# Attention stage of a two-layer backbone: one order for all units, the filler cut around the first transpositions

## The chip, the core and the metric
The kernel runs on one core of a Trainium2 chip. The metric is the device time of one execution, in microseconds (us); the time of a kernel is the median of several runs. Five engines work side by side, each through its own list of instructions: TensorE (PE, matrix products and transpositions), VectorE (DVE), ScalarE (ACT), GpSimd (POOL), and SyncE (SP), which here issues the DMAs. Results of TensorE go into PSUM, eight banks of 128 x 512 float32; everything else works from SBUF.

## The reference
Two layers over 1024 latent and 256 context tokens of width 1024: the first mixes tokens by differential attention, the second by a state-space scan; a squared-ReLU MLP follows each. The change lies in the attention:

```python
q_l = apply_rope(heads_qk(q_l), cos, sin) * scale       # 8 heads, two components of 64
k_all = jnp.concatenate([k_c, k_l], axis=1)             # 256 context + 1024 latent keys
def attend(q, k, v):
    s = jnp.einsum('bqhcd,bkhcd->bhcqk', q, k).astype(jnp.float32)
    p = jax.nn.softmax(s, axis=-1)
    w = p[:, :, 0] - lam * p[:, :, 1]                    # two softmaxes, one subtracted
    o = jnp.einsum('bhqk,bkhe->bqhe', w.astype(v.dtype), v)
    return rmsnorm(o, subln_g) * (1.0 - lambda_init)
y_lat = jnp.einsum('bte,ed->btd', o_l, w_o)
```
Context queries read the 256 context keys alone. All is float32.

## The kernel before
Products that need float32 accuracy are made of three (`mm3`, lines 132 to 134): both operands are held as a coarse part and a remainder, and three of the four cross products are summed in PSUM. `split` (lines 137, 138) makes the two parts: ScalarE copies the coarse one, VectorE or GpSimd subtracts it.

`phase_b` runs the attention in 72 units, nine for each head (the profile shows it from 224.1 to 858.5 us), and then five rounds without a unit of its own (n = 72 to 76). Unit 0 holds the 256 context queries against 256 keys, units 1 to 8 hold 128 latent queries each against 1280 keys. Each unit has these steps:

- `scores`: 8 or 12 products into banks 0 to 4 (lines 575, 581).
- `maxima` on VectorE (590, 594): reads the banks, writes the raw weights to SBUF with their extremes.
- `exps` on ScalarE (601, 604): two exponentials, one for each of the two softmaxes, with their sums.
- `combine` on VectorE (612, 613, 615): the weighted difference. L615 takes two operands from SBUF.

The weights have to stand the other way round for the product with the values. So TensorE transposes the weights of the unit before, in three parts (`w_part`, 622 and 627): four blocks into bank 5 (part 0), two into the second half of bank 6 (part 1), four into bank 7 where the unit has no group of filler, else into bank 5 again (part 2). Unit 0 of a head transposes unit 8 of the head before. The weights of a unit 0 have one part, of four blocks. `w_evac` empties a part into the coarse and remainder halves of `wT`: part 0 directly, by ScalarE (635) and VectorE (636); parts 1 and 2 by a copy on ScalarE (640) into one of three raw buffers and two steps of GpSimd (641 coarse, 642 remainder).

TensorE's work beside that, called filler, is of two kinds. `values` multiplies two finished units with the values: 30 products of 256 columns into the first half of bank 6, in units 1, 4, 6 and 8 (6 of them in unit 2 for the context queries); `pair_out` copies the sum out (725) and `pair_sums` adds its squares (732). And units 0, 1, 2, 3, 5 and 7 (table `AHEAD`) carry a projection group of the next head's queries or keys, 24 products into bank 7, of 512 columns, in units 1 and 3 of 256. The group is emptied at the unit's end: 256 columns by 523 and 524, 512 columns by 528 and 529, and then, one step at a time at the places of `next_post`, four DMAs and the sine (534, GpSimd), the sum (537, VectorE), the split and store (137, 138). Head 7 has no next head; it carries groups of the output product, 18 products of 512 columns, from n = 65 on.

PE, DVE, ACT and POOL run in written order (`manual_schedule`); the DMAs on SyncE are placed by the scheduler. The written order of a unit is: scores, maxima, all of `values`, then the three parts, each followed by its emptying, by one exponential (parts 0 and 1), by the combination (part 1), and by a slice of the group (`FILLS`, or products 0-2, 3-5, 6-7; `FILL_FIRST` puts unit 5's first slice ahead of part 0). In units with 30 products of values (`late`), all emptyings stand behind both exponentials and the combination. In the other units part 0 is emptied ahead of the first exponential, and part 1's copy stands ahead of the second.

Among the other work in the same lists: `norm_pair` (765 and a split, 137) of a finished head in units 7 to 2, `norm7` (801, 803) in the last head.

Of the kernel before, what the change touches and what calls it, by code (L numbers as in the profile page):

```python
# [70 lines left out]
class Prog:  # L71
# [575 lines left out]


    AHEAD = {0: (1, 0), 1: (1, 2), 2: (1, 1), 3: (0, 2), 5: (0, 0), 7: (0, 1)}
    FILLS = {1: (0, 0, 4, 8), 3: (0, 4, 8, 8)}  # L650
    FILL_FIRST = (5,)

    def b_start(self):

# [25 lines left out]
    def phase_b(self):  # L680
# [11 lines left out]
        pb = self.bank(6)  # L692
# [21 lines left out]
        def values(h, pair):  # L714
            V = loaded[h, "v"]
            last = 2 if pair == 0 else 10
            for kt in range(last):
                self.mm3(pb[:, 0:256], V[0][:, kt], V[1][:, kt], self.wT[0][:, kt], self.wT[1][:, kt],
                         kt == 0, kt == last - 1)

        hst = self.fv(7, 3, 8, 10)

# [33 lines left out]
        def norm_load(h, pair):  # L756
            i = nbuf.next()
            nloaded.append(i)
            self.dma(nbufs[i][0], self.od[h, :, 256 * pair : 256 * pair + 256])
            self.dma(nbufs[i][1], self.rsd[h, 2 * pair : 2 * pair + 2].rearrange("a b -> (a b)").partition_broadcast(128))  # L760

        def norm_pair(h, pair):
            i = nloaded.pop(0)
            (nob, nrb), (nhi, nlo) = nbufs[i], nsplit[i]
            nc.vector.scalar_tensor_tensor(nob, nob, self.sg, nrb, ALU.mult, ALU.mult)
            self.split(nhi, nlo, nob, nc.gpsimd)
            for j, t in enumerate((nhi, nlo)):
                self.dma(self.on[h, j, :, 256 * pair : 256 * pair + 256], t.bitcast(F32))
# [91 lines left out]
        prev, todo, sums, post, tail, run7 = None, [], [], [], [], []  # L860
# [4 lines left out]
        def next_post():  # L865
            f = post.pop(0) if post else None
            if f:
                f()

        ready = []  # L870

        def evac():
            while ready:
                self.w_evac(*ready.pop(0))

        with self.manual():
            for n in range(72 + 5):
                h, u = units[n] if n < 72 else (8, 9)
                front = n < 72
                groups = []  # L880
                pv = todo.pop(0)[1:] if todo and todo[0][0] == n else None
                late = pv and pv[1]
                parts = 3 if prev and prev[1] else 1 if prev else 0
                if front and n - 6 >= 9 and (n - 6) % 9 < 5 and (n - 6) // 9 < 7:
                    norm_load((n - 6) // 9 - 1, (n - 6) % 9)
                if h == 7 and u > 5:
                    load6(u)
                if front:
                    K = loaded[h, 'k', 0], loaded[h, 'k', 1]
                    pair = (u + 1) // 2  # L890
                    Q = loaded[h, pair]
                    s0 = hst[:, 0, h]
                    p, sn, sm = (p0.next(), p1), self.stat.next(), self.stat.next()
                    if u == 5 and h < 7:
                        load_v(h + 1)
                        load_k(h + 1, 0)
                        load_k(h + 1, 1)
                    if u % 2 == 0 and u < 8 and (h, pair + 1) not in loaded:
                        load_q(h, pair + 1)
                    if h < 7:  # L900
                        groups = [self.proj_group(h + 1, *a, wts[a[0]]) for a in (self.AHEAD[u],)] if u in self.AHEAD else []
                    self.scores(u, Q, K)
                    if u == 7 and h < 7:
                        load_q(h + 1, 0)
                    if u == 8 and h < 7:
                        load_q(h + 1, 1)
                    self.maxima(u, p, sm)
                if front:
                    if h < 7:
                        if u == 0:  # L910
                            qsplit = self.proj_weights(h + 1, 0)
                        if u == 5 and h < 6:
                            ksplit = self.proj_weights(h + 2, 1)
                if 65 <= n < 75:
                    groups = [wo_group(wo_order[n - 65])]
                fills = [[], [], []]
                if h >= 7 and groups:
                    fills = [groups[0][0][i : i + 2] for i in (0, 2, 4)]
                elif groups:
                    a = self.FILLS.get(u, (0, 3, 6, 8))  # L920
                    fills = [groups[0][0][a[i] : a[i + 1]] for i in range(3)]
                if pv:
                    values(*pv)
                if u in self.FILL_FIRST and front and h < 7:
                    for f in fills[0]:
                        f()
                    fills[0] = []
                for part in range(3):
                    if part < parts:
                        tb = pb[:, 256:512] if part == 1 else self.bank(7 if part == 2 and not groups else 5)  # L930
                        t = self.w_part(prev[1], prev[2], part, tb)
                        ready.append((*t, part == 0))
                    if not late or part == 2:
                        evac()
                    if part == 1:
                        next_post()
                    if front and part < 2:
                        self.exps(u, part, p, sm, s0, sn)
                    if front and part == 1:
                        if n - 7 >= 9 and (n - 7) % 9 < 5 and (n - 7) // 9 < 7:  # L940
                            norm_pair((n - 7) // 9 - 1, (n - 7) % 9)
                        self.combine(u, p, s0, sn)
                    if late and part == 1:
                        evac()
                    if part == 0:
                        todo7, run7 = run7, []
                        for f in todo7:
                            f.pop(0)()
                            if f:
                                run7.append(f)  # L950
                    if part == (2 if n < 73 else 0):
                        while sums and sums[0][0] <= n:
                            sums.pop(0)[1]()
                    for f in fills[part]:
                        f()
                if front and u == 0:
                    next_post()
                if pv:
                    pair_out(*pv)
                    sums.append((n + 1, lambda a=pv: pair_sums(*a)))  # L960
                    if pv[0] == 7:
                        tail.append((n + 1, pv[1]))
                next_post()
                if groups:
                    rest = groups[0][1]
                    rest[0]()
                    post += rest[1:]
                if h < 7 and u in (0, 2):
                    wts[0] = qsplit(u // 2)
                if h < 6 and u in (6, 7):  # L970
                    wk = ksplit(u - 6)
                if u == 8 and h < 6:
                    wts[1] = wk
                if front and u % 2 == 0:
                    todo.append((n + 2, h, pair))
                prev = (h, u, p[0]) if front else None
                if 0 < h < 8:
                    if u == 3:
                        newton = norm_calc(h - 1)
                    elif u == 4:  # L980
                        newton()
                    elif u == 5:
                        norm_rows(h - 1)
                if n == 72:
                    self.raw = Ring([self.wv(8, 1024), self.wv(12, 1024)])
                    self.wo_raws = [self.wo_load(3, 0), self.wo_load(0, 1)]
                if n == 60:
                    wload6(0)
                if n == 62:
                    wload6(1)  # L990
                    wload6(2)
                    wsplit6(0)
                if h == 7:
                    beside7(u)
                    if u > 5:
                        norm6(u)
                if tail and tail[0][0] == n:
                    run7.append(list(norm7(tail.pop(0)[1])))
# [1586 lines left out]
```

## Time and profile before

| | us |
|---|---|
| median of 3 runs | 2853.43 (2853.11 to 2854.3) |
| the profiled execution | 2849.43 |
| its span | 2847.7 |
| attention stage in it (224.1 to 858.5) | 634.4 |
| TensorE busy in that stage | 603.7 |
| VectorE, ScalarE, GpSimd busy in that stage | 509.8, 370.8, 411.7 |
| TensorE waiting for L636 in that stage | 23.9 in 16 waits |

The profile shows one execution. A row of a timeline has the start in us, the busy time, the engine, the line of the code, the operation, output and inputs with their shapes, how many equal instructions it joins, and, in brackets, the idle time of the engine ahead of it with the instruction that ended it. A row of stretches has the stretch, its length, and the busy time of PE, weight loading, DVE, ACT and POOL, then the granted clock of TensorE as a share of full speed, the share of DMA and GB/s. A row of waits has who waited for whom, the total, how often, and the longest. Matmuls of TensorE overlap: the distance between two starts, not the busy time of one, is what each adds. In the rows, F holds the weights and raw copies, R the queries, keys, values and `wT`, H and W projection weights and inputs, PS is PSUM.

### The profile page before, as it was taken

To read this page: it belongs to the slowest core of one execution; us is meant where nothing else is said; L and a number is where in the kernel's file an instruction comes from. 1 tells how busy PE (TensorE), PEld (TensorE's weight loads), DVE (VectorE), ACT (ScalarE), POOL (GpSimd) and SP (SyncE) were. 2 spreads that over 40 slices of the span, in tenths; PEclk is the share of its full clock that TensorE was granted. 3 is DMA by queue.
4 is the path that set the end of the run, shared out by engine and by line. 5 is a ranking of instruction groups with operands and counts; after the bars stand their busy time and mean duration, and the time that the engine had idled before them with its cause. 6 is when DMAs were issued, how large, how long until landed. Compare 5 with 4: busy or idle time off the path is not lost. (4 is left out here: it accounts for less than half of the span.)

```text
span 2847.7 us, 43378 instructions
## 1 busy us (share of the span) xinstructions
PE 2723.8 (96%) x15229; PEld 2284.8 (80%) x15229; DVE 2017.4 (71%) x2984; ACT 1368.4 (48%) x2583; POOL 1031.7 (36%) x901
## 2 busy tenths in 40 slices
PE   6999999999999999999999999889999999999999
PEld 4688888888877887778877878788887778878887
DVE  6366788888873676667698878799543697768466
ACT  3425555555653753333444445487344633344443
POOL 3314666666663600000030013588121143335414
PEclk9999999999999999999999999899999999999999
DMA  9956556555835359886799877579742244476544
GB/s 271 322 176 199 147 164 177 173 172 163 259 100 177 133 182 315 292 303 221 246 318 303 275 240 259 169 228 309 233 155 97 69 162 158 155 247 226 167 132 142
DMA packets 414823, 586.30 MB, mean 206 GB/s; under 512 B 41870, under 2 KB 260236, under 8 KB 411404
## 3 DMA queue, kind: packets, MB, share of 16 engines
q1 hardware_dynamic: 414604, 583.52, 63.8%
q8 instruction: 120, 1.97, 0.3%
q14 instruction: 99, 0.81, 0.1%
HBM read 396.38 MB, written 182.82 MB: 203 GB/s over the span
## 5 line engine op out<-in xcount | busy, mean ns | idle before, releaser
L132 PE MATMUL PS<-H 128*128 128x512 f32 x1072 | 420.9, 394 | 3.2 <-ACT H L137 1.9
L134 PE MATMUL PS<-H 128*128 128x512 f32 x1072 | 418.1, 391 | 2.0 <-DVE H L2260 1.3
L133 PE MATMUL PS<-H 128*128 128x512 f32 x1072 | 418.4, 390 | 0.0
L132 PE MATMUL PS<-H,R 128*128 128x512 f32 (+1 forms) x828 | 308.7, 375 | 4.4 <-ACT R L137 1.2
L133 PE MATMUL PS<-H,R 128*128 128x512 f32 (+1 forms) x828 | 299.0, 361 | 0.2 <-POOL H L138 0.2
L134 PE MATMUL PS<-H,R 128*128 128x512 f32 (+1 forms) x828 | 298.1, 361 | 0.0
L132 PEld LDWEIGHTS PS<-H 128*128 128x128 f32 x1072 | 201.6, 188 | 51.4 <-issue 6.2
L134 PEld LDWEIGHTS PS<-H 128*128 128x128 f32 x1072 | 201.6, 188 | 44.9 <-DVE H L2260 1.7
L133 PEld LDWEIGHTS PS<-H 128*128 128x128 f32 x1072 | 201.5, 188 | 40.5
L604 ACT ACTIVATE F<-F,stat 128x1280 f32<-128x1280 f32 x128 | 174.3, 1362 | 100.5 <-DVE F L594 100.3
L137 ACT ACTIVATE H<-U 128x640 fp32r<-128x640 f32 x216 | 131.9, 674 | 175.1 <-PE PS L133 145.6
L132 PE MATMUL PS<-R,H 128*128 128x512 f32 x520 | 208.4, 402 | 3.3 <-ACT H L137 3.3
L137 ACT ACTIVATE R<-W 128x512 fp32r<-128x512 f32 (+1 forms) x184 | 128.6, 707 | 168.8 <-PE PS L133 98.1
L134 PE MATMUL PS<-R,H 128*128 128x512 f32 x520 | 206.1, 398 | 1.8 <-DVE H L138 1.8
L133 PE MATMUL PS<-R,H 128*128 128x512 f32 x520 | 205.2, 395 | 0.0
L138 DVE TENSOR_TENSOR H<-U,H 128x640 fp32r<-128x640 f32 x216 | 165.4, 799 | 52.5 <-ACT H L137 51.3
L138 DVE TENSOR_TENSOR H<-W,H 128x512 fp32r<-128x512 f32 (+1 forms) x137 | 124.4, 918 | 102.0 <-ACT H L137 101.5
L594 DVE TENSOR_SCALAR_CACHE_REDUCE F<-PS 128x1280 f32<-128x1280 f32 x128 | 185.2, 1483 | 8.0 <-PE PS L581 7.7
L137 ACT ACTIVATE H<-W 128x512 fp32r<-128x512 f32 (+2 forms) x158 | 95.5, 613 | 189.0 <-PE PS L133 116.2
L132 PEld LDWEIGHTS PS<-H,R 128*128 128x128 f32 x828 | 157.7, 191 | 31.9 <-issue 4.1
L134 PEld LDWEIGHTS PS<-H,R 128*128 128x128 f32 x828 | 157.3, 190 | 25.6 <-issue 0.8
L641 POOL TENSOR_SCALAR R<-F 128x256 fp32r<-128x256 f32 (+1 forms) x128 | 126.2, 986 | 136.9 <-ACT F L640 123.1
(530 smaller groups left out, 6845.7 us busy)
## 6 DMA issues: line engine op xcount, KB each, us to landing
W<-in_mlp_w SPq DMA_DIRECT2D x176, 256.0 KB, 3.1
U<-Aa SPq DMA_DIRECT2D x108, 320.0 KB, 4.6
Aa<-FU SPq DMA_DIRECT2D x91, 320.0 KB, 4.5
Ad<-F SPq DMA_DIRECT2D x112, 256.0 KB, 2.8
W<-Ad SPq DMA_DIRECT2D x112, 256.0 KB, 2.7
FU<-in_mlp_w SPq DMA_DIRECT2D x32, 512.0 KB, 6.4
Ta<-FU SPq DMA_DIRECT2D x16, 1024.0 KB, 5.0
U<-in_ada_w SPq DMA_DIRECT2D x32, 512.0 KB, 9.1
```

Source lines behind the costliest of these rows:

```text
L132: mm(out, ah, bh, start=first, stop=False, **kw)
L133: mm(out, ah, bl, start=False, stop=False, **kw)
L134: mm(out, al, bh, start=False, stop=last, **kw)
L137: self.nc.scalar.activation(hi, src, AF.Copy)
L138: (lo_eng or self.nc.vector).tensor_tensor(lo, src, hi.bitcast(F32), ALU.subtract)
L594: ts(p[c], self.PS[:, 1280 * c : 1280 * c + 1280], 1.0, None, ALU.mult, ALU.min, accum_out=sm[:, c : c + 1])
L604: nc.scalar.activation(p[c], p[c], AF.Exp, bias=sm[:, c : c + 1], scale=-1.0, accum_out=sn[:, 0:1] if c else s0[:, u + 1 : u + 2])
L641: nc.gpsimd.tensor_scalar(hi, t, 1.0, 0.0, ALU.mult, ALU.add)
```

## The change
`FILLS`, `FILL_FIRST` and `late` go. `values` no longer issues its products but returns them, and all filler of a unit, the values ahead of the group, stands in one list `work`. A product of the values, or of a group of 256 columns, counts 1 there, one of 512 columns counts 2 (one "product" is the three of `mm3`). Up to a count of 6 is issued ahead of part 0 of the transpositions, up to 4 more behind part 0 with its emptying and the first exponential, and all the rest ahead of part 2. In every unit part 0 is emptied ahead of both exponentials, part 1's copy stands behind the second exponential, and part 2's copy last. In unit 0, `next_post` is called twice behind `pair_out`, no longer once at part 1.

```diff
@@ -647,8 +647,6 @@
 
 
     AHEAD = {0: (1, 0), 1: (1, 2), 2: (1, 1), 3: (0, 2), 5: (0, 0), 7: (0, 1)}
-    FILLS = {1: (0, 0, 4, 8), 3: (0, 4, 8, 8)}
-    FILL_FIRST = (5,)
 
     def b_start(self):
 
@@ -714,9 +712,8 @@
         def values(h, pair):
             V = loaded[h, "v"]
             last = 2 if pair == 0 else 10
-            for kt in range(last):
-                self.mm3(pb[:, 0:256], V[0][:, kt], V[1][:, kt], self.wT[0][:, kt], self.wT[1][:, kt],
-                         kt == 0, kt == last - 1)
+            return [lambda kt=kt: self.mm3(pb[:, 0:256], V[0][:, kt], V[1][:, kt], self.wT[0][:, kt], self.wT[1][:, kt],
+                                           kt == 0, kt == last - 1) for kt in range(last)]
 
         hst = self.fv(7, 3, 8, 10)
 
@@ -879,7 +876,6 @@
                 front = n < 72
                 groups = []
                 pv = todo.pop(0)[1:] if todo and todo[0][0] == n else None
-                late = pv and pv[1]
                 parts = 3 if prev and prev[1] else 1 if prev else 0
                 if front and n - 6 >= 9 and (n - 6) % 9 < 5 and (n - 6) // 9 < 7:
                     norm_load((n - 6) // 9 - 1, (n - 6) % 9)
@@ -913,53 +909,55 @@
                             ksplit = self.proj_weights(h + 2, 1)
                 if 65 <= n < 75:
                     groups = [wo_group(wo_order[n - 65])]
-                fills = [[], [], []]
-                if h >= 7 and groups:
-                    fills = [groups[0][0][i : i + 2] for i in (0, 2, 4)]
-                elif groups:
-                    a = self.FILLS.get(u, (0, 3, 6, 8))
-                    fills = [groups[0][0][a[i] : a[i + 1]] for i in range(3)]
-                if pv:
-                    values(*pv)
-                if u in self.FILL_FIRST and front and h < 7:
-                    for f in fills[0]:
+                work = [(1, f) for f in values(*pv)] if pv else []
+                if groups:
+                    work += [(1 if h < 7 and self.AHEAD[u][1] == 2 else 2, f) for f in groups[0][0]]
+
+                def fill(most=1000):
+                    while work and most > 0:
+                        cost, f = work.pop(0)
                         f()
-                    fills[0] = []
+                        most -= cost
+
+                fill(6)
                 for part in range(3):
+                    if part == 2:
+                        fill()
                     if part < parts:
                         tb = pb[:, 256:512] if part == 1 else self.bank(7 if part == 2 and not groups else 5)
-                        t = self.w_part(prev[1], prev[2], part, tb)
-                        ready.append((*t, part == 0))
-                    if not late or part == 2:
+                        ready.append((*self.w_part(prev[1], prev[2], part, tb), part == 0))
+                    if part == 0:
                         evac()
-                    if part == 1:
-                        next_post()
-                    if front and part < 2:
-                        self.exps(u, part, p, sm, s0, sn)
-                    if front and part == 1:
-                        if n - 7 >= 9 and (n - 7) % 9 < 5 and (n - 7) // 9 < 7:
-                            norm_pair((n - 7) // 9 - 1, (n - 7) % 9)
-                        self.combine(u, p, s0, sn)
-                    if late and part == 1:
-                        evac()
-                    if part == 0:
+                        if front:
+                            self.exps(u, 0, p, sm, s0, sn)
                         todo7, run7 = run7, []
                         for f in todo7:
                             f.pop(0)()
                             if f:
                                 run7.append(f)
+                        fill(4)
+                    elif part == 1:
+                        if u:
+                            next_post()
+                        if front:
+                            self.exps(u, 1, p, sm, s0, sn)
+                        evac()
+                        if front:
+                            if n - 7 >= 9 and (n - 7) % 9 < 5 and (n - 7) // 9 < 7:
+                                norm_pair((n - 7) // 9 - 1, (n - 7) % 9)
+                            self.combine(u, p, s0, sn)
+                    else:
+                        evac()
                     if part == (2 if n < 73 else 0):
                         while sums and sums[0][0] <= n:
                             sums.pop(0)[1]()
-                    for f in fills[part]:
-                        f()
-                if front and u == 0:
-                    next_post()
                 if pv:
                     pair_out(*pv)
                     sums.append((n + 1, lambda a=pv: pair_sums(*a)))
                     if pv[0] == 7:
                         tail.append((n + 1, pv[1]))
+                if u == 0:
+                    next_post()
                 next_post()
                 if groups:
                     rest = groups[0][1]
```

No instruction of PE, DVE, ACT or POOL is added or removed in the stage. Three places show what moves; the names in them are regions of SBUF (F_1851 holds the weights and their raw copies, R_110 `wT`, queries and stores, R_1850 the keys, H the group's inputs), and a line above 647 is 2 to 3 lower in the code after.

TensorE in unit 0 of head 3, before, from the scores on:

```order
L575 MATMUL PS<-R_1850,R_110 128x256 x8
L627 MATMUL PS<-ident,F_1851 128x128 x4
L132 MATMUL PS<-H,R_110 128x512
L133 MATMUL PS<-H,R_110 128x512
L134 MATMUL PS<-H,R_110 128x512
```

and after:

```order
L575 MATMUL PS<-R_1850,R_110 128x256 x8
L132 MATMUL PS<-H,R_110 128x512
L133 MATMUL PS<-H,R_110 128x512
L134 MATMUL PS<-H,R_110 128x512
L132 MATMUL PS<-H,R_110 128x512
L133 MATMUL PS<-H,R_110 128x512
L134 MATMUL PS<-H,R_110 128x512
L132 MATMUL PS<-H,R_110 128x512
L133 MATMUL PS<-H,R_110 128x512
L134 MATMUL PS<-H,R_110 128x512
L627 MATMUL PS<-ident,F_1851 128x128 x4
```

Three products of the group (bank 7) have moved from behind the four transpositions of part 0 to ahead of them.

ScalarE from unit 8 of head 2 to part 0 of unit 0 of head 3, before:

```order
L604 ACTIVATE F_1851,FC<-F_1851,stat 128x1280
L604 ACTIVATE F_1851,stat<-F_1851,stat 128x1280
L137 ACTIVATE W<-W 128x256
L635 ACTIVATE R_110<-PS 128x4x128
L640 ACTIVATE F_1851<-PS 128x256
L640 ACTIVATE F_1851<-PS 128x512
L725 ACTIVATE FC<-PS 128x256
L635 ACTIVATE R_110<-PS 128x4x128
```

and after:

```order
L635 ACTIVATE R_110<-PS 128x4x128
L604 ACTIVATE F_1851,FC<-F_1851,stat 128x1280
L604 ACTIVATE F_1851,stat<-F_1851,stat 128x1280
L640 ACTIVATE F_1851<-PS 128x256
L137 ACTIVATE W<-W 128x256
L640 ACTIVATE F_1851<-PS 128x512
L722 ACTIVATE FC<-PS 128x256
L635 ACTIVATE R_110<-PS 128x4x128
```

Unit 8's part 0 (first L635) is emptied ahead of both exponentials; the copies of its parts 1 and 2 keep their places behind them, the norm's split (L137 on W) now between them. On VectorE L636 moves likewise from behind L615 to ahead of the norm's L765 (762 after) and of L612, L613 and L615.

TensorE at the end of unit 2 and the start of unit 3 of the same head, before:

```order
L627 MATMUL PS<-ident,F_1851 128x128 x4
L732 MATMUL PS<-lamc,adat 128x1 x2
L132 MATMUL PS<-H,R_110 128x512
L133 MATMUL PS<-H,R_110 128x512
L134 MATMUL PS<-H,R_110 128x512
L132 MATMUL PS<-H,R_110 128x512
L133 MATMUL PS<-H,R_110 128x512
L134 MATMUL PS<-H,R_110 128x512
L581 MATMUL PS<-R_1850,R_110 128x512 x4
L581 MATMUL PS<-R_1850,R_110 128x256 x4
L581 MATMUL PS<-R_1850,R_110 128x512 x4
L627 MATMUL PS<-ident,F_1851 128x128 x4
```

and after:

```order
L627 MATMUL PS<-ident,F_1851 128x128 x4
L729 MATMUL PS<-lamc,adat 128x1 x2
L581 MATMUL PS<-R_1850,R_110 128x512 x4
L581 MATMUL PS<-R_1850,R_110 128x256 x4
L581 MATMUL PS<-R_1850,R_110 128x512 x4
L132 MATMUL PS<-H,R_110 128x256
L133 MATMUL PS<-H,R_110 128x256
L134 MATMUL PS<-H,R_110 128x256
L132 MATMUL PS<-H,R_110 128x256
L133 MATMUL PS<-H,R_110 128x256
L134 MATMUL PS<-H,R_110 128x256
```

The last two products of unit 2's group no longer stand between its part 2 and the scores of unit 3, and in unit 3 its own group follows the scores directly, where part 0 stood.

## The prediction

> **What bounds the kernel now.** I read the page's engine line, the waits of TensorE in the attention stage (224 to 860 us, the only part in which the order differs), the stretches of its units, and last the timelines of all engines around the units where TensorE waits.
>
> ```profile
> PE 2723.8 (96%) x15229; PEld 2284.8 (80%) x15229; DVE 2017.4 (71%) x2984; ACT 1368.4 (48%) x2583; POOL 1031.7 (36%) x901
> ```
> ```profile
> PE PS L627 <- DVE R L636: 22.7, 15, 2.6
> ...
> PE PS L627 <- DVE FC L803: 1.9, 3, 0.8
> ...
> PE PS L133 <- DVE R L636: 1.2, 1, 1.2
> ```
> (waits: who, for whom, us in total, times, longest). TensorE is the bound, so a us counts only if TensorE waits it. The one large wait is that of the transpositions (L627) for the remainder of the first bank's emptying (L636), because both of their places lie in bank 5. Unit 0 of heads 1 to 6 (its length, TensorE's busy time, and as the last column but two the granted clock):
>
> ```profile
> 295.50:305.40 9.90, 8.31 (x49) 7.02 (x48) 7.33 (x20) 5.74 (x19) 8.07 (x10) 1.00 0.60 176
> 372.50:385.00 12.50, 9.89 (x49) 8.26 (x47) 9.00 (x22) 6.92 (x21) 9.48 (x11) 0.86 0.71 216
> 452.00:463.00 11.00, 8.39 (x50) 7.04 (x48) 7.89 (x20) 6.69 (x21) 8.84 (x10) 1.00 0.77 214
> 530.00:542.30 12.30, 9.70 (x50) 8.15 (x48) 8.84 (x22) 6.91 (x21) 9.83 (x12) 0.86 0.70 216
> 609.30:620.20 10.90, 8.28 (x49) 6.99 (x47) 7.78 (x20) 6.53 (x21) 8.73 (x10) 1.00 0.72 213
> 687.30:698.20 10.90, 8.27 (x48) 6.96 (x47) 7.78 (x20) 6.52 (x21) 8.75 (x10) 1.00 0.76 211
> ```
> Together 67.5 us. Twice the clock fell to 0.86 behind the wait, which made these units 1.4 us longer than the others with the same wait. Around one of them (unit 8 begins at 445.1):
>
> ```profile
> 451.99 1.20 PE L575 MATMUL PS<-R,R 128*128 128x256 f32 x8
> 455.79 0.66 PE L627 MATMUL PS<-ident,F 128*128 128x128 f32 x4 [2.61 <-DVE R L636]
> 458.37 0.38 PE L627 MATMUL PS<-ident,F 128*128 128x128 f32 x2
> ...
> 449.81 1.36 ACT L604 ACTIVATE F<-F,stat 128x1280 f32<-128x1280 f32 x1 [3.37 <-DVE F L594]
> ...
> 452.58 0.40 ACT L137 ACTIVATE W<-W 128x256 fp32r<-128x256 f32 x1
> 452.89 0.57 ACT L635 ACTIVATE R<-PS 128x512 fp32r<-128x512 f32 x1
> 453.37 0.86 ACT L640 ACTIVATE F<-PS 128x256 f32<-128x256 f32 x2
> ...
> 453.16 1.97 DVE L615 SCALAR_TENSOR_TENSOR F<-F,stat 128x1280 f32<-128x1280 f32 x1
> 455.06 0.68 DVE L636 TENSOR_TENSOR R<-PS,R 128x512 fp32r<-128x512 f32 x1
> ```
>
> **The change part by part.** No instruction is added or removed; only places change. A product of 512 columns is issued every 0.23 us (9 of them and four transpositions between 455.79 and 458.37), one of 256 every 0.12 (half of it).
>
> *Unit 0, heads 1 to 6.* L636 now stands ahead of the combination L615, and the filler ahead of the transpositions. But the filler writes bank 7, which unit 8's last copy (the second L640) must have read. In unit 8 now: scores 2.3, 18 products of the values 2.2, so transpositions at 4.5; from transpositions to L635 0.63 (rows of unit 3 below), so L635 at 5.1; exponentials at 5.6 and 7.0 (0.49 behind L635 by the same rows, and 1.4 further, 1.36 of it busy); copy at 8.4, norm split 8.65, second copy 8.95 to 9.55. Unit 0's scores end at 6.9 + 1.0 = 7.9. TensorE waits 1.7 there, not 2.6. The combination ends at 10.9, when TensorE is still in the filler (to 11.7): no second wait. Length: the first product 2.65 behind the unit's start, and from there the work that took from the released transpositions to the next unit's start now (455.79 to 463.0, 7.2): 9.85; head 1 has no norm split, 9.5. Sum 58.75 against 67.5: **-8.7**, the clock's two falls included, since head 1 kept 1.00 after a wait of 1.7. Bounds: -3 (the clock falls in four heads) to -10.
>
> *Unit 5, heads 1 to 6.* The second use of bank 5 waited 0.76 and cost about 1.0 with its ramp:
>
> ```profile
> 504.19 0.66 PE L627 MATMUL PS<-ident,F 128*128 128x128 f32 x4 [0.76 <-DVE R L636]
> ```
> Now 15 products lie between both uses (3.5 us against L635 and L636 in 0.63 + 1.3): gone, **-6.0**; none of this can turn into a loss.
>
> *Unit 3, heads 0 to 6.* Units 2, 3 and 4:
>
> ```profile
> 480.02 0.60 PE L627 MATMUL PS<-ident,F 128*128 128x128 f32 x4
> ...
> 482.29 2.49 PE L581 MATMUL PS<-R,R 128*128 128x512 f32 x12
> 484.62 0.60 PE L627 MATMUL PS<-ident,F 128*128 128x128 f32 x4
> ...
> 488.95 2.57 PE L581 MATMUL PS<-R,R 128*128 128x512 f32 x12
> ...
> 480.65 0.60 ACT L640 ACTIVATE F<-PS 128x512 f32<-128x512 f32 x1 [0.48 <-PE PS L627]
> ...
> 481.47 0.65 ACT L137 ACTIVATE R<-FC 128x512 fp32r<-128x512 f32 x1
> ...
> 485.25 0.60 ACT L635 ACTIVATE R<-PS 128x512 fp32r<-128x512 f32 x1 [1.65 <-PE PS L627]
> 485.75 1.36 ACT L604 ACTIVATE F<-F,stat 128x1280 f32<-128x1280 f32 x1
> ...
> 488.83 0.60 ACT L640 ACTIVATE F<-PS 128x512 f32<-128x512 f32 x1
> ...
> 482.24 1.09 DVE L138 TENSOR_TENSOR R<-FC,R 128x512 fp32r<-128x512 f32 x1
> 483.45 0.69 DVE L529 SCALAR_TENSOR_TENSOR FC<-PS,W 128x512 f32<-128x512 f32 x1
> ...
> 489.30 1.55 DVE L615 SCALAR_TENSOR_TENSOR F<-F,stat 128x1280 f32<-128x1280 f32 x1
> ...
> 487.55 0.40 POOL L641 TENSOR_SCALAR R<-F 128x256 fp32r<-128x256 f32 x1 [1.24 <-ACT F L640]
> 488.04 0.73 POOL L642 TENSOR_TENSOR R<-F,R 128x256 fp32r<-128x256 f32 x1
> 489.52 1.82 POOL L641 TENSOR_SCALAR R<-F 128x512 fp32r<-128x512 f32 x1 [0.74 <-ACT FC L733]
> 491.42 1.30 POOL L642 TENSOR_TENSOR R<-F,R 128x512 fp32r<-128x512 f32 x1
> ```
> Unit 2's last transpositions stood 2.27 ahead of unit 3 (480.02 to 482.29); behind all of the filler they stand 0.8 ahead. On ScalarE the copy follows by 0.63, the store's split L137 by 1.45 and 0.65: done 1.3 after unit 3's start. On VectorE L138 (1.2 with its issue) and L529 (0.7) follow, so bank 7 is free at 3.2; unit 3's filler, now directly behind its scores (2.33), waits 0.9. Bounds 0.3 (L138 in 0.6) to 1.5 (held as below). I take 1.1, nearer the row's own durations: 7 x 1.1 = **+7.7**.
>
> *Unit 4, heads 0 to 6.* Counted from unit 3's first transpositions, now 2.2 ahead of unit 4 (before, 488.95 - 484.62 = 4.3): L635 at 0.63, exponentials 1.12 and 2.53, both copies 3.9 to 4.75, where the first stood between the exponentials. GpSimd starts its first pair at 4.3; L615 runs from 4.45 to 6.0. A GpSimd copy of 512 took 1.82 beside L615 at 489.52 and ended 0.5 behind it, one of 256 alone took 0.40: so the first L642 ends near 6.8, the second L641 near 7.5, its L642 (1.30) at 8.8. The values of unit 4 need that remainder for their seventh block: 2.2 + 2.33 + 18 x 0.12 + 0.36 + 0.12 = 7.2. TensorE waits 1.6, in two pieces. Before, the same remainder ended at 492.72, 0.9 ahead of its need. Bounds 0.2 (no hold: 0.62 for L641, the chain ends at 7.3) to 1.8. 7 x 1.6 = **+11.2**.
>
> *Unit 2 of head 0.* Unit 1 there is short, and its transpositions move from 2.3 to 4.5:
>
> ```profile
> 233.73 2.47 PE L581 MATMUL PS<-R,R 128*128 128x512 f32 x12
> ...
> 239.35 2.49 PE L581 MATMUL PS<-R,R 128*128 128x512 f32 x12
> ...
> 240.44 1.55 DVE L615 SCALAR_TENSOR_TENSOR F<-F,stat 128x1280 f32<-128x1280 f32 x1
> 241.91 0.42 DVE L524 SCALAR_TENSOR_TENSOR R<-PS,R 128x256 fp32r<-128x256 f32 x1
> ```
> L635 5.1, exponentials 5.6 and 7.0, L615 at 9.0 (before 6.7), L524 to 10.8, which is 5.2 behind unit 2's start; its filler wants bank 7 at 3.05: **+2.2** (0 to 2.5).
>
> *Head 7.* The waits for L636 there (1.2 in unit 2, 0.4 in unit 4, 1.7 in unit 8) and half of those for L803 (0.8 twice) go, with ramps some 6; behind unit 8 the output group waits for its bank's copy instead (1.6), and unit 2 for the weights' remainder (0.9): **-3.6** (-7 to 0).
>
> *At nothing:* L537 behind the combination in unit 0 (VectorE idled 2.2 there, off TensorE's path; if the store gets later, unit 1 has 9.2 us of work as cover); the wait of L636 for L635 ahead of the combination (VectorE idles 1.1 there, what queues behind are L765 and the combination, which wait for the exponentials anyway); SyncE's loads, which move by two or three places (only the first unit and head 7's unit 1 wait for one).
>
> Sum: -8.7 - 6.0 + 7.7 + 11.2 + 2.2 - 3.6 = **+2.8 us**. Against the profiled execution's 2849.4 this gives 2852.2; that execution lies 4.0 under the median of the runs, 2853.4, so by the median 2856.
>
> A rule weighed here is that of the Trainium skill, "SBUF — State Buffer", section "Who interferes with whom": a VectorE instruction with two SBUF inputs and a GpSimd instruction that reads SBUF exclude each other, and whichever issues first holds the port for its whole length. The trace shows it in L641 (0.40 alone, 1.82 beside L615); L138, also with two SBUF inputs, took 1.09 beside a GpSimd copy begun earlier, but that one was itself held by L615. By the rule L138 would now meet a free-running L642 and wait: 1.5 and not 1.1 in unit 3, a sum of +5.6.
>
> **The rivals.**
> *The copies keep up (faster).* For it: units 3 and 4 run without a wait now, and GpSimd is busy 36%. If GpSimd is not held by L615 and L529 comes in time, units 3 and 4 cost 0.3 a head: -8.7 - 6.0 + 2.1 + 2.2 - 3.6 = -14.0, 2839. It decides at a remainder that ends within 7.3 of unit 3's transpositions. Against: the 1.82. Chance 0.25.
> *The lateness runs on (slower).* One cause: GpSimd and VectorE hold each other longer than I count, so the copies' second halves end 0.5 later in every unit. For it: the 1.82; unit 6 takes its values behind the same chain and has only 0.2 left by the same count. Price: units 3 and 4 at their upper bounds (+2.8 and +1.4), 0.5 in unit 6 of seven heads (+3.5) and in four units of head 7 (+2.0); unit 8's miss is absorbed by unit 0's wait. +2.8 + 9.7 = +12.5, 2866. It decides from 0.2 later on. Against: in units 6 and 8 the first bank was already emptied late, and their values never waited. Chance 0.19.
> *The clock falls at the new waits.* At 2.6 it fell in two heads of five, at 1.7 in none of one. If it does at unit 0 in all six, 6 x 1.4 = +8.4: 2865. Chance 0.06. The Trainium skill, "TensorE: Matmul & The Clock Gate", section "HAM oscillation — how this bites in real kernels", asks for an idle gap above about 3.4 us; the trace differs, with two falls after 2.6.
> *My forecast,* gains and new waits of one size: chance 0.50, 2849 to 2863 by itself.
>
> **How the numbers follow.** The predicted time is 2856. A measurement here tells 0.2%, 5.7 us, from no change: 2847.7 to 2859.1. Faster: the first rival all but 0.01, and 0.02 of mine, 0.26. Slower: the second and third and 0.11 of mine (unit 3 at 1.5 or unit 4 at 1.8 and head 7 gaining less), 0.36. Same: 0.38. The range reaches into the first rival and to the end of the second: 2841 to 2867.
>
> **What would show it.** Right: in the waits of TensorE no L627 for L636 in heads 1 to 6; instead L132 for L640 about 1.7 in unit 0, L132 for L529 about 1 in unit 3, values (L133) for GpSimd's L642 in unit 4, 1 to 2 in two pieces; 0.86 gone from the six stretches. Wrong: units 3 and 4 still at 6.7 and 7.0, or L615 beginning no later than now relative to its unit; or waits in units 6 and 7.

## The result: slower by 1.5%, and the profile after

The changed kernel takes 2897.76 us (median of 4 runs, 2886.25 to 2900.75) against 2853.27 of the kernel before; the ratio is 1.0153 (95% interval 1.0121 to 1.0184). The forecast was 2856, with a range of 2841 to 2867. The profiled execution took 2900.75 us, its span is 2898.9: 51.2 longer than the span shown of before, of which 49.5 lie between the starts of the first and the last of the 72 units (a unit starts with the first product of its scores).

The engine line of the page after, and the longest waits of TensorE in the attention stage (who for whom, total, times, longest):

```profile
PE 2747.2 (95%) x15229; PEld 2298.3 (79%) x15229; DVE 2023.5 (70%) x2984; ACT 1365.0 (47%) x2583; POOL 1045.7 (36%) x901
```
```profile
PE PS L729 <- ACT F L640: 16.9, 18, 1.7
PE PS L132 <- ACT F L640: 10.8, 6, 1.9
PE PS L134 <- POOL R L138: 5.0, 7, 0.9
PE PS L132 <- DVE FC L529: 4.5, 7, 0.9
...
PE PS L627 <- DVE R L636: 3.4, 7, 0.5
...
PE PS L748 <- ACT FC L730: 2.5, 7, 0.4
PE PS L133 <- POOL R L642: 2.4, 5, 0.5
...
PE PS L132 <- DVE R L524: 2.0, 1, 2.0
```
The one large wait of before (L627 for L636, 22.7) has become many. The largest is new and was nowhere in the forecast: the sums of squares (`pair_sums`, L729 here) wait for a copy of weights, L640. Head 3 shows where; the stretches are its units 0, 2, 3, 4 and 5, with TensorE's granted clock as the last column but two:

```profile
474.10:484.20 10.10, 8.24 (x49) 6.87 (x47) 7.92 (x22) 6.43 (x19) 7.54 (x9) 1.00 0.74 194
493.60:503.60 10.00, 10.00 (x58) 8.50 (x57) 8.68 (x14) 4.81 (x11) 4.98 (x5) 1.00 0.84 268
503.60:515.40 11.80, 8.19 (x53) 6.82 (x52) 6.87 (x11) 6.34 (x13) 6.72 (x8) 0.96 0.55 166
515.40:525.00 9.60, 9.60 (x54) 8.83 (x54) 6.39 (x11) 2.29 (x5) 4.58 (x4) 0.70 0.31 85
525.00:535.40 10.40, 9.79 (x55) 7.96 (x53) 7.94 (x13) 7.68 (x17) 8.00 (x8) 1.00 0.36 100
```
Unit 3 took 6.7 us before and 11.8 now; unit 4 waits for nothing and still takes 9.6 where it took 7.0, at a clock of 0.70. At the end of unit 2 and inside unit 3, the timelines of TensorE, ScalarE, VectorE and GpSimd:

```profile
503.60 2.56 PE L581 MATMUL PS<-R,R 128*128 128x512 f32 x12
506.81 0.38 PE L132 MATMUL PS<-H,R 128*128 128x256 f32 x1 [0.64 <-DVE FC L529]
...
509.66 0.39 PE L134 MATMUL PS<-H,R 128*128 128x256 f32 x1 [0.92 <-POOL R L138]
...
510.24 0.60 PE L627 MATMUL PS<-ident,F 128*128 128x128 f32 x4
...
512.25 0.66 PE L627 MATMUL PS<-ident,F 128*128 128x128 f32 x4 [0.48 <-DVE R L636]
514.48 1.02 PE L729 MATMUL PS<-lamc,adat 128*128 128x1 f32 x4 [1.57 <-ACT F L640]
```
```profile
501.90 0.37 ACT L640 ACTIVATE F<-PS 128x256 f32<-128x256 f32 x1
...
510.87 0.60 ACT L635 ACTIVATE R<-PS 128x512 fp32r<-128x512 f32 x1 [4.98 <-PE PS L627]
511.37 1.35 ACT L604 ACTIVATE F<-F,stat 128x1280 f32<-128x1280 f32 x1
...
512.71 1.35 ACT L604 ACTIVATE F<-F,stat 128x1280 f32<-128x1280 f32 x1
...
514.06 0.86 ACT L640 ACTIVATE F<-PS 128x256 f32<-128x256 f32 x2
```
```profile
504.92 1.03 DVE L138 TENSOR_TENSOR R<-FC,R 128x512 fp32r<-128x512 f32 x1 [0.82 <-ACT R L137]
...
508.08 0.08 DVE L594 DVE_READ_ACCUMULATOR F<-PS 128x1 f32 x1
```
```profile
502.36 0.41 POOL L641 TENSOR_SCALAR R<-F 128x256 fp32r<-128x256 f32 x1 [4.62 <-ACT F L640]
502.85 1.85 POOL L642 TENSOR_TENSOR R<-F,R 128x256 fp32r<-128x256 f32 x1
504.66 0.74 POOL L138 TENSOR_TENSOR F<-F 128x256 fp32r<-128x256 f32 x1
...
508.32 1.28 POOL L138 TENSOR_TENSOR R<-W,R 128x512 fp32r<-128x512 f32 x1
```
Read it as a chain. The group of the filler stands ahead of part 0 and waits twice: for bank 7 (L529) and, at its fifth product, for the remainder of the second half of its weights (L138 on GpSimd, which ends at 509.6). That L138 is the last piece of a queue on GpSimd without a pause: its first piece, at 502.36, had waited 4.62 for part 1's copy of unit 2 (L640 at 501.90), which now stands behind both exponentials, and its second, L642, took 1.85 beside the combination on VectorE (L615, 502.48 to 504.10). So part 0 is transposed at 510.24, 6.6 behind the unit's start. ScalarE has been idle for 4.98 us: the maxima of the first exponential were there at 508.2, but L635 stands ahead of it in ScalarE's order and needs part 0. The exponentials then take 2.7, part 1's copy (L640) stands behind them, and the sums, which write into the same bank as part 1, wait 1.57 for it. Each engine hands on the lateness of the one before, and TensorE pays twice, at the head of the chain and at its end.

### The profile page after: what moved, and what is told of

It is laid out like the page before. It is cut to its first block, busy times and chain, and to the rows that moved or that the text cites. A ratio compares the mean times of both kernels' runs of the same rounds, so it can differ in the third digit from the quotient of the medians.

```text
span 2898.9 us, 43355 instructions
## 1 busy us (share of the span) xinstructions
PE 2747.2 (95%) x15229; PEld 2298.3 (79%) x15229; DVE 2023.5 (70%) x2984; ACT 1365.0 (47%) x2583; POOL 1045.7 (36%) x901
## 5 line engine op out<-in xcount | busy, mean ns | idle before, releaser
L132 PE MATMUL PS<-H 128*128 128x512 f32 x1072 | 420.5, 393 | 2.0 <-DVE F L1503 1.0
L133 PE MATMUL PS<-H 128*128 128x512 f32 x1072 | 417.7, 390 | 0.0
L132 PE MATMUL PS<-H,R 128*128 128x512 f32 (+1 forms) x828 | 306.0, 372 | 21.1 <-ACT F L640 10.8
L133 PE MATMUL PS<-H,R 128*128 128x512 f32 (+1 forms) x828 | 298.8, 361 | 0.0
L132 PEld LDWEIGHTS PS<-H 128*128 128x128 f32 x1072 | 201.2, 188 | 49.6 <-issue 6.1
L133 PEld LDWEIGHTS PS<-H 128*128 128x128 f32 x1072 | 201.3, 188 | 40.7
L137 ACT ACTIVATE H<-U 128x640 fp32r<-128x640 f32 x216 | 132.0, 675 | 170.1 <-PE PS L133 142.9
L132 PE MATMUL PS<-R,H 128*128 128x512 f32 x520 | 206.6, 398 | 4.8 <-ACT H L137 3.3
L137 ACT ACTIVATE R<-W 128x512 fp32r<-128x512 f32 (+1 forms) x184 | 128.9, 707 | 171.4 <-PE PS L133 104.4
L133 PE MATMUL PS<-R,H 128*128 128x512 f32 x520 | 204.1, 393 | 2.6 <-POOL R L138 2.6
L132 PEld LDWEIGHTS PS<-H,R 128*128 128x128 f32 x828 | 157.4, 190 | 53.3 <-ACT F L640 12.4
L138 DVE TENSOR_TENSOR H<-U,H 128x640 fp32r<-128x640 f32 x216 | 165.6, 800 | 48.5 <-ACT H L137 47.4
L138 DVE TENSOR_TENSOR H<-W,H 128x512 fp32r<-128x512 f32 (+1 forms) x137 | 128.5, 948 | 98.1 <-ACT H L137 97.6
L594 DVE TENSOR_SCALAR_CACHE_REDUCE F<-PS 128x1280 f32<-128x1280 f32 x128 | 185.6, 1483 | 11.9 <-PE PS L581 11.9
L642 POOL TENSOR_TENSOR R<-F,R 128x256 fp32r<-128x256 f32 (+1 forms) x128 | 188.9, 1476 | 10.7
L137 ACT ACTIVATE H<-W 128x512 fp32r<-128x512 f32 (+2 forms) x158 | 95.5, 613 | 187.9 <-PE PS L133 114.2
L604 ACT ACTIVATE F<-F,stat 128x1280 f32<-128x1280 f32 x128 | 173.4, 1359 | 11.6 <-DVE F L594 11.6
```

Source lines behind the costliest of these rows:

```text
L132: mm(out, ah, bh, start=first, stop=False, **kw)
L133: mm(out, ah, bl, start=False, stop=False, **kw)
L137: self.nc.scalar.activation(hi, src, AF.Copy)
L138: (lo_eng or self.nc.vector).tensor_tensor(lo, src, hi.bitcast(F32), ALU.subtract)
L594: ts(p[c], self.PS[:, 1280 * c : 1280 * c + 1280], 1.0, None, ALU.mult, ALU.min, accum_out=sm[:, c : c + 1])
L604: nc.scalar.activation(p[c], p[c], AF.Exp, bias=sm[:, c : c + 1], scale=-1.0, accum_out=sn[:, 0:1] if c else s0[:, u + 1 : u + 2])
```

## The experiments

Ratios are to the kernel before, which ran beside each group of runs (medians 2854.6, 2852.8 and 2854.6 us). Theory F holds the place of the filler to be the cause, theory C the place of the copies. "Unit" times are from the first product of its scores to that of the next.

**The filler's order alone, with the emptying of before.** Edit: `work` and `fill` as in the change; around them `if not late or part == 2: evac()` ahead of the exponential again.

> The changed order of TensorE's filler alone; the emptying of the weights' parts stays as before (late units behind the combination, part 1's copy between the exponentials). Theory F (the place of the filler costs: ahead of part 0 it runs into bank 7 and into the weights' remainder L138, 0.8 and 1.1 us in unit 3, and holds up part 0 and with it the exponentials): unit 3 near 9.9 us where it was 6.66 before and 11.75 after, no fall of the clock behind it, 2868 to 2880 us in all. Theory C (the place of the copies costs): near the kernel before, 2845 to 2857 us, unit 3 near 7.

2876.78 us, ratio 1.0081 (1.0063 to 1.0099). Units 3 and 4 of head 3 take 9.05 and 7.01, at full clock:

```profile
493.40:502.40 9.00, 7.69 (x52) 6.32 (x51) 6.02 (x8) 4.98 (x11) 4.84 (x5) 1.00 0.65 185
```
The time lies in theory F's range. Unit 3 is 0.9 shorter than the theory said, and unit 5, which it did not name, is longer than before (11.15 against 10.59). The place of the filler alone costs half of the loss; the other half needs the new emptying as well.

**The emptying alone, with the filler's order of before.** Edit, in the loop of before (the calls of `next_post` move as in the change):

```diff
-                    if not late or part == 2:
+                    if part != 1:
                         evac()
...
                         self.exps(u, part, p, sm, s0, sn)
+                    if part == 1:
+                        evac()
```

> The changed emptying alone (part 0 ahead of both exponentials in all units, part 1's copy behind the second); the filler stands as before. Theory F: unit 3 starts with part 0 and has about 5 us of TensorE work behind it, against some 4.2 us until part 1's copy is done, so the sums of squares don't wait; unit 5 loses its wait of 0.76; 2838 to 2850 us. Theory C: the sums of squares in unit 3 wait 1 to 1.7 us for part 1's copy as they do after, and the clock falls behind it: 2880 to 2898 us.

2917.26 us, ratio 1.0222 (1.0203 to 1.0240): slower than the whole change, outside both ranges, and for a reason that neither theory had. Unit 3 is healthy (7.2, sums hardly wait); units 0, 5 and 7 are not (13.8, 12.8, 12.2). The waits, and unit 8 of head 3 with the start of the next unit 0:

```profile
PE PS L627 <- DVE F L615: 45.9, 16, 3.9
```
```profile
564.45 1.25 PE L627 MATMUL PS<-ident,F 128*128 128x128 f32 x10
565.46 1.20 PE L575 MATMUL PS<-R,R 128*128 128x256 f32 x8
570.52 0.65 PE L627 MATMUL PS<-ident,F 128*128 128x128 f32 x4 [3.86 <-DVE F L615]
```
```profile
565.09 0.60 ACT L635 ACTIVATE R<-PS 128x512 fp32r<-128x512 f32 x1 [4.51 <-PE PS L627]
565.58 1.35 ACT L604 ACTIVATE F<-F,stat 128x1280 f32<-128x1280 f32 x1
```
Unit 8 has 30 products of values. They stand ahead of part 0 in this order, so part 0 comes 5.9 us into the unit, and the exponentials, which must now let L635 pass, start at 7.0 (565.58 against the unit's start at 558.56) where they started at 4.7 before. The combination L615 is late by as much, and the next unit's first transpositions wait 3.86 for it. So the emptying ahead of the exponentials ties ScalarE to TensorE's position: it may only stand there if part 0 comes early and without waits. The cut of the filler is what makes it bearable in units 4, 6 and 8, and the filler's own waits are what breaks it in unit 3.

**One thing undone: part 1's copy between the exponentials.** Edit: `evac()` moved ahead of `exps(u, 1, ...)`.

> The changed kernel with one thing undone: part 1's copy stands between the exponentials again, in all units. The copy then ends some 1.4 us earlier, so the wait of the sums in unit 3 shrinks from 1.73 to 0.3, and unit 4 runs at full clock again. Theory F: the waits for bank 7, for the weights' remainder and for L636 in unit 3 stay (0.8, 1.1, 0.65), so 2864 to 2874 us. Theory C: they are side effects of late copies and go too: 2845 to 2860 us.

2870.70 us, ratio 1.0061 (1.0046 to 1.0076), within theory F's range. Unit 3 falls to 9.1, unit 4 to 7.0. The waits:

```profile
PE PS L627 <- DVE R L636: 3.4, 7, 0.5
...
PE PS L729 <- ACT F L640: 2.4, 8, 0.7
...
PE PS L134 <- POOL R L138: 1.1, 5, 0.2
```
In unit 3 of head 3 the waits for bank 7 and for L636 stay (0.45 and 0.48), but that for the weights' remainder falls from 0.92 to 0.23, as the wait at the sums does from 1.57. Here theory C was right and F was not: that wait came in good part from the copy's late place in unit 2, which held up GpSimd: its first L642 starts earlier, is done before L615 begins, and takes 0.74 instead of 1.85. The place of this copy is worth 27 us in the changed order, and 10 once unit 3 begins with part 0 and part 2 has bank 5 (below).

**The sums into other columns.** Edit: `pair_sums` writes columns 0 and 1 of bank 6 where these are free.

> The changed kernel, order untouched, but the sums of squares go into the first half of bank 6 (free by then) in units 3, 5, 7 and 0, so that they need not wait for part 1's copy. Both theories lose the 16.9 us of these waits. Theory F: the clock stops falling, 2862 to 2878 us, with unit 3 near 9.5 to 10 us. Theory C: the late copies hold GpSimd's chain, and the values of unit 4 wait 1 to 1.6 us for the second halves instead: 2878 to 2892 us.

2898.58 us, ratio 1.0151 (1.0136 to 1.0166): nothing changed, as neither theory expected, because the wait itself stayed to the tenth:

```profile
PE PS L730 <- ACT F L640: 16.9, 18, 1.7
```
The order between the two engines was kept here for the whole bank, whatever the columns. The Trainium skill says as much ("PSUM — Partial Sum Buffer", section "PSUM bank collisions raise a hardware error": the compiler adds a dependency between instructions of different engines that touch the same bank and quadrant of partitions, at any address); the trace agrees, 16.9 in 18 waits with either set of columns. The experiment took nothing away, so it tells nothing about the theories.

**Unit 3 with part 0 first.** Edit: `if pv or u != 3: fill(6)`.

> The changed kernel, but unit 3 issues no filler ahead of part 0 (four products behind part 0, the rest ahead of part 2). Theory: since part 0's emptying stands ahead of the exponentials, whatever TensorE waits for ahead of part 0 (bank 7, the weights' remainder: 1.9 us in unit 3) is handed to the exponentials, to part 1's copy behind them and so to the sums of squares (1.73 more) and to the clock in unit 4. With part 0 first, unit 3 goes from 11.75 to 6.7 to 7.2 us and unit 4 from 9.6 to 7.0, 48 us less in all heads together: 2848 to 2856 us. The prediction's own term would still come: the values of unit 4 wait 1.6 us for GpSimd, 2860 to 2866 us. Rival, the copy behind both exponentials is too late by itself: the sums in unit 3 still wait over 1 us and the clock still falls, 2875 us or more.

2870.90 us, ratio 1.0061 (1.0041 to 1.0082). Unit 3 falls to 8.24 and unit 4 to 7.0, the sums no longer wait there, and the clock stays up. All units together take 31.0 us less, not the 48 I gave: bank 7 and the weights' remainder still cost 0.19 and 0.70 us of idle time in unit 3, and unit 2 of the last head grew by 4.1 beside it. Neither the 1.6 in unit 4 that I had predicted nor the rival's 2875 came.

**Part 2 always into bank 5.** Edit: `self.bank(5)`.

> The changed kernel, but part 2 always goes into bank 5, so that the first products of a following unit's group (bank 7) need not wait for its copy. Theory: the 10.8 us of waits of unit 0 for L640 go, unit 0 falls from 10.1 to 8.0 to 8.3 us, unit 3 and 4 stay as they are: 2880 to 2889 us. Rival: the wait moves on to part 0 of unit 0 (for the copy in bank 5 or for the combination of unit 8), unit 0 stays at 9 to 10 us: 2890 to 2900 us.

2884.03 us, ratio 1.0117 (1.0091 to 1.0143). Unit 0 of heads 1 to 6 falls from 10.1 to 8.0, without a wait; but the wait moves one unit ahead, where part 2 of unit 8 now waits for part 0's emptying in bank 5, and unit 8 grows from 7.75 to 9.3.

```profile
PE PS L627 <- DVE R L636: 12.9, 15, 1.3
```
The time lies in the range that I gave, but in part by luck: of the 14.0 us that unit 0 gains in six heads, unit 8 gives back 10.0; another 9.0 come from unit 4, where the clock fell in three heads and not in six, although the waits of unit 3 are within 0.04 us the same.

**Both.**

> Both: unit 3 with part 0 first, part 2 always in bank 5; copies behind both exponentials as in the changed kernel. If the two waits are independent: 2836 to 2845 us, faster than the kernel before. If one wait only takes the place of the other (values for GpSimd in unit 4, part 0 of unit 0 for the combination): 2850 to 2865 us.

2862.05 us, ratio 1.0029 (1.0018 to 1.0040). Singly the two edits took 26.9 and 13.7 us from the changed kernel, together they take 35.7; the 9.0 that unit 4's clock gave to the second were in the first as well. The time lies in the range of the second case, but neither wait that I named for it is there (unit 4 takes 7.0, unit 0 8.0). My lower number took more from each edit than it had to give: unit 8 keeps its 9.3, unit 3 its 8.2.

**Both, and the copy between the exponentials.**

> As the run before it, and part 1's copy between the exponentials again. If the place of the copy alone costs something once the other waits are gone, this is faster by 2 to 10 us: units 3 and 5 without their waits of 0.3 to 0.4 at the sums, values of unit 8 without 0.7. If not, both are the same within 3 us.

2852.19 us, ratio 0.9996 (0.9986 to 1.0006): the place of the copy is worth another 10 us, mostly in unit 3 (7.29, without any wait in heads 2 to 6), unit 8 (8.8) and unit 2 (10.0); unit 4 grows to 8.0, where part 2 now waits for L636 in bank 5. So the whole loss of the change goes with three edits of places.

**Exponentials first, in unit 3 alone.** TensorE's order is that of the changed kernel. Edit: in unit 3 both `exps` ahead of part 0's `evac()`.

> The changed kernel, but in unit 3 both exponentials stand ahead of part 0's emptying; TensorE's order is untouched, so its waits ahead of part 0 (bank 7, the weights' remainder) stay. Theory (part 0 ahead of the exponentials hands TensorE's lateness to them, they to part 1's copy, that to the sums of squares, that to the clock): the wait of the sums in unit 3 falls from 1.73 to under 0.4, unit 4 comes back from 9.6 to 7.0, 2865 to 2875 us. Rival (the waits come from GpSimd or VectorE being late, whatever ScalarE's order): unit 3 and 4 as in the changed kernel, 2890 to 2900 us.

2877.05 us, ratio 1.0075 (1.0053 to 1.0097), where the changed kernel has 1.0153; that is 2 us above the range of the theory and far below the rival's. Unit 3 of head 3, on ScalarE:

```profile
501.14 1.36 ACT L604 ACTIVATE F<-F,stat 128x1280 f32<-128x1280 f32 x1 [2.29 <-DVE F L594]
...
503.91 0.58 ACT L635 ACTIVATE R<-PS 128x512 fp32r<-128x512 f32 x1
504.74 0.38 ACT L640 ACTIVATE F<-PS 128x256 f32<-128x256 f32 x1 [0.25 <-PE PS L627]
```
```profile
PE PS L729 <- ACT F L640: 3.1, 9, 0.7
```
The exponentials now follow their maxima (the release is L594), the copy follows TensorE, the sums in unit 3 wait for nothing, unit 3 takes 9.57 and unit 4 7.0. One exchange on one engine, with the waits at the head of the chain left as they were (0.63 for bank 7, 0.92 for the weights), gives nearly half of the loss back: this is the link that the chain needed.

**A mended order.** Part 0 directly behind the scores in units 1 and 3 without values; part 2 into bank 5 except in unit 4; the copy between the exponentials; in unit 2 of head 7 the group behind part 1.

> The changed order with what the runs so far point to: part 0 directly behind the scores in units 1 and 3 without values, part 2 into bank 5 except in unit 4, part 1's copy between the exponentials, and in unit 2 of head 7 the group behind part 1. By the units of the run with bank 5 and the copy between (640.4 us of stage): unit 2 of head 0 -3.7, unit 2 of head 7 -3.5, units 4 and 5 -0.45 in six heads: about 630 us, 2841 to 2848 us. If the filler behind part 0 in unit 1 of head 0 and unit 2 of head 7 only shifts the waits: as that run, 2852 us.

2848.29 us, ratio 0.9981 (0.9970 to 0.9991). Unit 2 of head 0 lost its wait (9.7) and unit 4 came back to 7.0, while unit 5 stayed at 10.1; unit 2 of head 7 gained nothing (14.7).

**The same with L636 between the two maxima in unit 8.**

> As the mended order, and in unit 8 VectorE empties part 0 (L636) between the two maxima, no longer behind both. Part 2 of unit 8 waits 1.28 us for L636 in bank 5; the second exponential gets its maxima 0.7 later, of which 0.35 shows. If that wait is L636's place behind the maxima: unit 8 from 8.8 to 7.3 to 7.6, 2833 to 2841 us. If the wait moves on to the combination or to unit 0: within 3 us of the mended order.

2849.55 us, ratio 0.9981 (0.9970 to 0.9991). Unit 8 falls from 8.8 to 7.4, and unit 0 grows from 8.2 to 10.0, because the second exponential and with it the combination are later:

```profile
PE PS L627 <- DVE F L615: 14.5, 8, 3.8
```
**The kernel before with the filler of unit 0 alone.** Edit:

```diff
-    FILL_FIRST = (5,)
+    FILL_FIRST = (0, 5)
```

> The kernel before with one thing from the change: unit 0's first three products of the group ahead of part 0 (no other unit, no emptying moved). The wait of 2.6 us for L636 turns into one for unit 8's last copy in bank 7, done some 2.2 us behind unit 0's start, so 1.2 us: unit 0 from 10.97 to 9.4 to 9.7 and without falls of the clock, 2840 to 2846 us. If part 0 then waits for the combination as well: 2848 to 2854 us.

2847.51 us, ratio 0.9975 (0.9965 to 0.9986). Unit 0 came to 9.5 as expected, without a fall of the clock; 1.1 us in unit 2 of each of five heads was given back, where the values now wait for L636:

```profile
PE PS L133 <- DVE R L636: 7.7, 6, 3.7
...
PE PS L132 <- ACT F L640: 5.7, 6, 1.1
```
One line thus gives as much as the whole mended order. Both are faster than the kernel before, by 0.2%, and than the changed one. Between the two profiled executions, though, the units differ by only 1.6 of the 7.1 us between the medians: unit 0 gives 11.6, unit 2 of heads 1 to 6 takes 5.8 and head 7 takes 4.8, most of it a wait of 3.7 for L636 in its unit 2. Where the rest lies is open. Ahead of the stage, where no order differs, the traces of these kernels differ by up to 6.0 us.

## Why the prediction was wrong, step by step

The units of the two profiled executions, summed, against the terms of the forecast:

| term | forecast | measured |
|---|---|---|
| unit 0, heads 1 to 6 | -8.7 | -5.5 |
| unit 5, heads 1 to 6 | -6.0 | -1.2 |
| unit 3, heads 0 to 6 | +7.7 | +33.5 |
| unit 4, heads 0 to 6 | +11.2 | +14.5 |
| unit 2, head 0 | +2.2 | +2.2 |
| head 7 (measured to the start of its last unit) | -3.6 | +2.1 |
| unit 8, heads 0 to 6 | 0 | +4.7 |
| sum of these | +2.8 | +50.3 |

**Unit 3 is the step that failed.** I found its first wait, L132 for L529, and placed it rightly (the product comes 3.2 us behind the unit's start, as forecast; 0.64 us of idle time here, 4.5 in seven). But I booked it as one wait and ended there. Two things were left out. The group's fifth product needs weights whose remainder GpSimd makes behind unit 2's parts; I followed bank 7 and not the other input (0.92 of idle time, most of it from the copy's new place in unit 2, as the run with the copy between the exponentials shows). And everything that stands behind the waiting product was not followed: part 0, L635, the exponentials, the copy, the sums. I named the copy's new place and never asked who waits for it on bank 6. The exchange in unit 3 alone shows that link.

**Unit 4** came out near its number for a wrong reason. The values did not wait for GpSimd's L642 there at all: with unit 3 grown, its part 0 stood 5.1 us ahead of unit 4 and not 2.2. The 14.5 us are the clock: unit 4 ran at 0.70 behind a unit 3 with four waits. The rival of a falling clock was there, but tied to unit 0, and had a chance of 0.06. In the runs that take the wait at the sums away, unit 4 runs at full clock. The waits do not settle it, though: with part 2 always in bank 5 they all stay, and unit 4 is at 7.0 in four heads of seven. The wait for L642 was real and in unit 8 (2.4 us in five).

**Unit 0** worked as described: no wait for L636, one for L640, 2.0 us and not 1.7 in heads 2 to 6 (by the distance of two issues), 1.7 in head 1, and one fall of the clock. Unit 8 itself had grown by 0.8, for which the forecast had nothing.

**Unit 5** lost its wait of 0.76, as said, but got two others: 0.3 us of idle time for the sums behind L640 and 0.4 for the transposition of the norms (L748) behind L730. "None of this can turn into a loss" was true of the wait and not of the unit.

**Head 0's unit 2** was right to the tenth (L132 for L524, 2.0). **Head 7** gained nothing: in its unit 2 the output group waits twice for GpSimd's remainders of the weights (L133 for L138, 2.6 together).

The second rival (lateness that runs on) had the sign and the idea; its size of +12.5 was wrong, and its engine for the most part. The lateness ran through ScalarE's order; GpSimd and VectorE holding each other is in it only by the L642 of 1.85 us, ahead of the weights' remainder. On L138 the port rule that I weighed shows, but decided nothing: begun on VectorE at 504.92, it ends 0.55 behind the GpSimd instruction that ran when it began (504.66 to 505.40). That was not the L642 that I feared, and L138 took 1.03 us, no longer than before; there too it ended 0.5 behind the GpSimd copy beside it.

## What to carry to other kernels

Before an instruction is moved ahead of others in an in-order queue, ask when its input comes in every unit, not in the one that it is meant to help: behind it, all the rest of that queue is as late as the slowest input. A wait that the new order creates on the bounding engine is not priced by its own length; follow what stands behind it on that engine, through the engines that it feeds, back to the next place where the bounding engine needs them. And look for the smallest part of a change that brings its gain: here a kernel with one more entry in a table is 0.25% faster, and the general rule around it cost 1.5%.

## What was unexpected of the hardware

The clock's falls are a matter of chance at one length of wait. In unit 0 of heads 2 to 6 the same wait of 1.9 to 2.0 us (the distance of two issues, less its usual value) stood in six kernels: the unit took 1.6 us longer than its neighbours, with the clock at 0.85, in 11 of 30 cases (1 of 5 in the changed kernel, 4 of 5 with the copy between, none of 5 with L636 between the maxima). Two examples, units 0 of heads 3 and 4 in the changed kernel with the copy between:

```profile
462.30:472.30 10.00, 8.23 (x48) 6.87 (x47) 8.76 (x22) 6.50 (x20) 8.54 (x10) 1.00 0.70 211
542.00:553.60 11.60, 9.81 (x49) 7.94 (x47) 7.93 (x20) 6.51 (x20) 8.70 (x10) 0.85 0.74 221
```
Waits of 1.2 to 1.7 in unit 0 never did it, those of 2.8 in the kernel before in 2 of 5 cases, and those of 4.0 always (6 of 6, the emptying alone). The Trainium skill, "TensorE: Matmul & The Clock Gate", section "What's actually happening", describes a window that runs free of the kernel, which fits the chance; it asks for an idle window of some 3.4 us, which the falls behind 2.0 do not fit. By these counts, as an estimate, a wait of 2 us on TensorE costs about 2.6 on average here (2.0 + 11/30 x 1.6). The four executions of the changed kernel differ by 14.5 us, with a mean granted clock of 0.985 in the shortest and 0.981 in the longest; that such falls make the whole difference was not tested.
